# Part of an FFN's up projection as seven block products, three down chunks, the residual in DRAM, and new planner costs

## The chip, the cores and the metric

One core of a Trainium2 chip runs the whole program. The metric is the device time in microseconds (us) of one execution; the kernel before takes 1389.71 us, the median of three runs.

## The reference, cut to what matters

Two decoder layers on an input of 512 tokens x 1024 features, all in float32. Each layer is a mixer (layer 0: a gated state-space scan and stick-breaking attention; layer 1: an mLSTM) with a residual sum, followed by a gated conv FFN with a residual sum:

```python
def conv_ffn(h, up_w, conv_w, conv_b, down_w):
    u = causal_dwconv(h @ up_w, conv_w, conv_b)
    gate, val = jnp.split(u, 2, axis=-1)
    return (jax.nn.silu(gate) * val) @ down_w
...
        h = h + conv_ffn(rmsnorm(h, norm_w[layer, 1]), ffn_up_w[layer], ffn_conv_w[layer],
                         ffn_conv_b[layer], ffn_down_w[layer])
```

`up_w` is 1024 x 5632, that is 22 gate tiles and 22 value tiles of 128 features; `down_w` is 2816 x 1024. The conv has width 3.

## The kernel before, in words

Activations lie feature by token: a tile is 128 features x 512 tokens, the residual `h` is 8 such tiles. A float32 product is made of three fast ones (`mm3`): each operand is split into a rounded part hi (a cast on ACT) and the rest lo (a subtraction on VectorE, called DVE), and PE multiplies hi by hi, hi by lo and lo by hi. Weights come from DRAM as units of up to 128 x 1024 elements (`load_unit`, on SP's queue, into two `raw` buffers), are split in `split_weights` into tiles hi and lo with five buffers of each, and are asked for ahead by `prefetch`. All other tiles come from one pool of 71 slots.

The FFN (`ffn`, line 1174) follows the list `FFN_PLAN`. An entry "up" j makes the gate tile j and the value tile 22 + j: `feat` runs 8 x 3 matmuls of 512 columns for each; DVE reads the PSUM and multiplies it with the row `rb` of the norm, giving u; ACT scales u into c; DVE adds the other two taps of the conv; ACT takes the SiLU of the gate, and DVE multiplies the two. The result is one tile of the down projection's input.

The down projection takes tiles in chunks of 8 (0 to 7, 8 to 15). Within a chunk it uses a scheme of seven block products: two input tiles and two output tiles, with the 512 tokens halved, form a 2 x 2 block product, which seven products of 256 columns give in place of eight. `token_sums` makes the sums of token halves of a pair of tiles (F, G, and the splits B, s, Fh, Fl, Gh, Gl), once per pair; `weight_tiles` makes the sums of weight blocks: P1 and P3 by two DMAs each, the second of which accumulates and is issued by POOL, P2 and P4 by DVE. `down_blocks` (line 1227) runs the products for the two output tiles 2c and 2c + 1, for c of 0 to 3, and adds them to `h`, which stays in its slots, straight from PSUM. Three PSUM tiles are used, X, Z and Y; X takes four products one on top of the other and is read in between, Y two. So a product that goes on in X or Y has to wait for the reader of the one before. The tiles 16 to 21 go plainly (`down_rest`, six per output tile, 512 columns).

The order of instructions is set by a planner. `Recorder` collects all calls; `cost` (line 288) gives each a duration; `order` simulates the five engines, with latencies between them, buffers and PSUM, and always issues on each engine the earliest call in program order that is ready. The program is then written out in that order, fixed for each engine. The four lines below set how far weights can run ahead, and how many slots there are:

```python
W_BUFS = 5
RAW_BUFS = 2
SLOTS = 71
SLOT = 520
```

Of the kernel before, what the change touches and what calls it, by code (L numbers as in the profile page):

```python
# [84 lines left out]
def _ffn_units(i, l):  # L85
# [3 lines left out]
    for kind, n in FFN_PLAN:  # L89
        if kind == "up":  # L90
# [6 lines left out]
        else:  # L97
# [175 lines left out]
class Recorder:  # L273
# [15 lines left out]
    def cost(c):  # L289
# [25 lines left out]
        return 60 + 2.0 * n  # L315
# [133 lines left out]
class Net:  # L449
# [65 lines left out]
    def weight_tiles(self):  # L515

        v = self.nc.vector
        while self.wi < len(self.sizes):
# [655 lines left out]
    def ffn(self, l, h, last):  # L1174
        nc = self.nc
        xs, _, _, rb = self.norm(h, f"nw{l}1")
        pairs, ss, first = {}, [], None
        for kind, j in FFN_PLAN:
            if kind == "down":
                a, b = CHUNKS[j]  # L1180
                for c in range(4):
                    self.down_blocks([pairs[k] for k in range(a // 2, b // 2)], h, c)
                continue
            if kind == "rest":
                self.down_rest(ss, h, last)
                continue
            cc = []
            for part in range(2):
                n = j + part * FF
                ps = self.ps(("pj", "zz", "yy")[self.n % 3])  # L1190
                self.feat(ps, xs)
                u, c = self.slot("u"), self.slot("c")
                nc.vector.tensor_tensor(u, ps, rb, op=ALU.mult)
                nc.scalar.activation(c, u, AF.Identity, scale=self.param(f"fw{l}2", n), bias=self.param(f"fb{l}", n))
                for d in (1, 2):
                    nc.vector.scalar_tensor_tensor(c[:, d:T], u[:, 0 : T - d], self.param(f"fw{l}{2 - d}", n), c[:, d:T],
                                                   op0=ALU.mult, op1=ALU.add)
                cc.append(c)
            nc.scalar.activation(cc[0], cc[0], AF.Silu)
            nc.vector.tensor_tensor(cc[1], cc[0], cc[1], op=ALU.mult)  # L1200
# [7 lines left out]
    def token_sums(self, c1, c2):  # L1208
# [3 lines left out]
        t = self.slot("B11", F32R)  # L1212
        self.nc.scalar.copy(t[:, a], c1[:, a])
        v.tensor_tensor(t[:, b], c1[:, a], t[:, a].bitcast(F32), op=ALU.subtract)
# [269 lines left out]
```

## Time and profile before

| | us |
|---|---|
| median of 3 runs (1389.37 to 1391.11) | 1389.71 |
| the profiled execution | 1389.56 |
| its span, first to last instruction | 1387.8 |
| PE (TensorE matmuls) busy | 1376.7 |
| DVE (VectorE) busy | 1116.2 |
| ACT (ScalarE) busy | 783.9 |
| POOL (GpSimd) busy | 87.1 |

The granted TensorE clock was 1.000 over the span. The first FFN runs from about 453 to 811 us, the second from about 1026 to the end; before the first lie the state-space scan and the attention, between the two the mLSTM. Busy times of an engine are a union: where two instructions overlap, the time counts once, so the sum of their durations is longer. Matmuls overlap so much that only the distance of their starts says how fast they go. All matmuls and nearly all other instructions have the line of the helper that issues them, L436 (L446 in the changed kernel), so groups are told apart by their tiles.

### The profile page before, as it was taken

The numbers are of one execution on the slowest core, as the hardware profiler recorded it, in microseconds if no ns is written. First come the engines' busy times: TensorE is split into PE (matmuls) and PEld (weight loads), VectorE is DVE, ScalarE is ACT, GpSimd is POOL, SyncE is SP. The second block draws the span as 40 slices with busy tenths as digits, with TensorE's granted clock in tenths as the row PEclk, the third lists the DMA queues.
The fourth block names the chain that finished last, engine by engine and source line by source line (L and its number), as shares of the span: only waits on it lengthen the run. The fifth ranks groups of instructions, "written<-read, shape, count | busy, mean of one in ns | idle before, by whom it ended". The sixth has DMA issues, their size and how long they took to land.

```text
span 1387.8 us, 20206 instructions
## 1 busy us (share of the span) xinstructions
PE 1376.7 (99%) x7491; PEld 1185.3 (85%) x7491; DVE 1116.2 (80%) x1963; ACT 783.9 (56%) x1325; POOL 87.1 (6%) x172
## 2 busy tenths in 40 slices
PE   9999999999999999999999999999999999999998
PEld 8898998989788888988898898888888899889887
DVE  7999889999997778878877657798758886888662
ACT  7798997786665444344434446776434444444440
POOL 0000001201120001000100000110000010010000
PEclk9999999999999999999999999999999999999999
DMA  6423223223312345243532225222234354443422
GB/s 220 130 77 112 86 78 98 70 83 132 98 46 91 101 127 137 92 138 113 129 122 95 81 82 171 77 92 89 65 106 126 102 129 129 122 133 95 137 68 84
DMA packets 53617, 147.96 MB, mean 107 GB/s; under 512 B 6136, under 2 KB 7160, under 8 KB 53520
## 3 DMA queue, kind: packets, MB, share of 16 engines
q1 hardware_dynamic: 48912, 138.29, 31.4%
q0 software_dynamic: 4608, 8.39, 3.7%
q8 instruction: 59, 0.97, 0.3%
q14 instruction: 38, 0.31, 0.1%
HBM read 141.36 MB, written 2.15 MB: 103 GB/s over the span
## 4 chain that ended last, share of the span: by engine, by line
PE 88%; DVE 5%; issue 3%; ACT 3%; POOL 1%; DMA 0%; SPq 0%; DVEq 0%; POOLq 0%; ACTq 0%
PE pj L436 43%; PE yy L436 26%; PE zz L436 14%; PE tt L436 5%; DVE gt L436 1%; DVE wt L436 1%; DVE lo L436 1%; DVE wTl L436 0%; ACT L436 0%; ACT Kh L436 0%; DMA h<-in_xT 0%; POOL wt L436 0%; ACT Q L436 0%; DVE ss L436 0%; ACT hi L436 0%
## 5 line engine op out<-in xcount | busy, mean ns | idle before, releaser
L436 ACT CAST hi<-raw 128x1024 fp32r<-128x1024 f32 (+2 forms) x236 | 227.8, 968 | 257.2 <-PE yy L436 58.6
L436 DVE TENSOR_TENSOR lo<-raw,hi 128x1024 fp32r<-128x1024 f32 (+2 forms) x236 | 263.8, 1120 | 25.2 <-ACT hi L436 24.5
L436 PE MATMUL pj<-xnh,hi 128*128 128x512 f32 x488 | 194.1, 398 | 0.0
L436 PE MATMUL pj<-xnh,lo 128*128 128x512 f32 x488 | 193.9, 397 | 0.0
L436 PE MATMUL pj<-xnl,hi 128*128 128x512 f32 x488 | 193.5, 396 | 0.0
L436 DVE SCALAR_TENSOR_TENSOR c<-u,pp,c 128x511 f32<-128x511 f32 (+2 forms) x212 | 158.0, 748 | 3.9 <-ACT c L436 1.6
L436 PE MATMUL yy<-xnl,hi 128*128 128x512 f32 x320 | 126.4, 395 | 0.0
L436 PE MATMUL yy<-xnh,lo 128*128 128x512 f32 x320 | 126.2, 394 | 0.0
L436 PE MATMUL yy<-xnh,hi 128*128 128x512 f32 x320 | 125.6, 392 | 0.0
L436 PE MATMUL pj<-lo,xnh 128*128 128x384 f32 (+2 forms) x320 | 108.6, 340 | 0.0
L436 PEld LDWEIGHTS pj<-xnh,lo 128*128 128x128 f32 x488 | 91.8, 188 | 19.1
L436 PEld LDWEIGHTS pj<-xnl,hi 128*128 128x128 f32 x488 | 91.8, 188 | 18.9
L436 PEld LDWEIGHTS pj<-xnh,hi 128*128 128x128 f32 x488 | 91.9, 188 | 18.8 <-issue 0.2
L436 PE MATMUL pj<-hi,xnl 128*128 128x384 f32 (+2 forms) x320 | 107.2, 336 | 0.0
L436 PE MATMUL pj<-hi,xnh 128*128 128x384 f32 (+2 forms) x320 | 106.8, 338 | 0.0
L436 ACT ACTIVATE c<-u,pp 128x512 f32<-128x512 f32 x100 | 81.1, 813 | 9.7 <-DVE u L436 8.3
L436 PE MATMUL zz<-xnl,hi 128*128 128x512 f32 x184 | 72.7, 395 | 0.0
L436 PE MATMUL zz<-xnh,lo 128*128 128x512 f32 x184 | 72.5, 394 | 0.0
L436 PE MATMUL zz<-xnh,hi 128*128 128x512 f32 x184 | 72.2, 392 | 0.0
L436 PEld LDWEIGHTS yy<-xnh,hi 128*128 128x128 f32 x320 | 60.2, 188 | 14.0
L436 PEld LDWEIGHTS yy<-xnl,hi 128*128 128x128 f32 x320 | 60.1, 188 | 13.9
L436 PEld LDWEIGHTS yy<-xnh,lo 128*128 128x128 f32 x320 | 60.1, 188 | 13.3
(418 smaller groups left out, 3330.7 us busy)
## 6 DMA issues: line engine op xcount, KB each, us to landing
raw<-in_w SPq DMA_DIRECT2D x168, 512.0 KB, 3.4
raw<-in_w SPq DMA_DIRECT2D x44, 384.0 KB, 3.1
P<-in_w SPq DMA_DIRECT2D x32, 256.0 KB, 5.6
P<-in_w POOLq DMA_DIRECT2D x32, 256.0 KB, 6.8
h<-in_xT SPq DMA_DIRECT2D x16, 256.0 KB, 4.7
E<-acsd SPq DMA_DIRECT2D x16, 256.0 KB, 3.9
raw<-in_w SPq DMA_DIRECT2D x16, 256.0 KB, 3.1
raw<-in_w SPq DMA_DIRECT2D x8, 264.0 KB, 2.7
```

The source lines that it names most:

```text
L436: getattr(getattr(nc, c.engine), c.method)(*(r(a) for a in c.args), **{k: r(v) for k, v in c.kw.items()})
```

## The change

It does five things.

1. In each FFN five of the 22 gate/value pairs (7, 10, 13, 16, 19) are made in block form: the two output tiles are gate j and value j, the inputs the eight feature tiles in four pairs. `up_blocks` copies four of the seven products from PSUM with ACT (two of them negated), adds or subtracts three with DVE, and then multiplies both u with `rb`. The sums of the input's token halves (entries "x" of the plan) need the weighted input itself, `hw`, which DVE makes anew; two of the seven operands are the splits that there are already.
2. The down projection has three chunks of 6 tiles (0 to 5, 6 to 11, 12 to 17), so three tile pairs per product, and four tiles are left for `down_rest`.
3. The residual lies in DRAM during the FFN (`hd`): 8 tiles are stored after the norm, each chunk loads two tiles per set and stores them again, and `down_rest` loads all eight.
4. The weight units of a block are as wide as the block needs (`raw` and P tiles of 768, 384 or 1024, 512 columns).
5. The planner's costs are changed: matmuls 0.4414 ns per column and 5 ns, scans 2.04 ns per element, POOL's power 250 + 190 ns per element, masks 330 + 0.6 ns.

```diff
-CHUNKS = [(0, 8), (8, 16)]
-REST = 16
-FFN_PLAN = [("up", j) for j in range(9)] + [("down", 0)] + [("up", j) for j in range(9, 17)] + [("down", 1)]
-FFN_PLAN += [("up", j) for j in range(17, FF)] + [("rest", 0)]
+CHUNKS = [(0, 6), (6, 12), (12, 18)]
+REST = 18
+UP_BLOCKS = (7, 10, 13, 16, 19)
+FFN_PLAN = [("up", 0), ("up", 1), ("x", 0), ("up", 2), ("x", 1), ("up", 3), ("x", 2), ("up", 4), ("x", 3), ("up", 5)]
+FFN_PLAN += [("load", 0), ("up", 6), ("down", 0)] + [("up", j) for j in range(7, 12)]
+FFN_PLAN += [("load", 1), ("up", 12), ("down", 1)] + [("up", j) for j in range(13, 18)]
+FFN_PLAN += [("load", 2), ("up", 18), ("down", 2)] + [("up", j) for j in range(19, FF)] + [("rest", 0)]
...
             if c.ins[0].base.dt == F32R:
-                return max(n / 2.4 + 2.5, m * 0.84)
-            return max(4 * n / 2.4 + 5, 3.4 * m)
+                return max(n * 0.4414 + 5, m * 0.84)
+            return max(4 * n * 0.4414 + 5, 3.4 * m)
...
+            if c.method == "tensor_tensor_scan":
+                rate = 2.04
...
-        return 60 + 2.0 * n
+        if c.method == "tensor_tensor":
+            return 250 + 190 * n
+        return 330 + 0.6 * n if c.method == "affine_select" else 100
...
-            r1, r2 = self.raw_tile(), self.raw_tile()[:, 0:kb]
+            r1, r2 = self.raw_tile()[:, 0 : 2 * kb], self.raw_tile()[:, 0:kb]
...
-            p1, p2, p3, p4 = (self.slot(f"P{k}") for k in (1, 2, 3, 4))
+            p1, p2, p3, p4 = (self.slot(f"P{k}", n=kb) for k in (1, 2, 3, 4))
...
+        hd = [self.dram.tile([P, T], F32, name=self.name("hd")) for _ in range(KD)]
+        for k in range(KD):
+            nc.sync.dma_start(hd[k], h[k])
...
+        def load(c):
+            loaded[c] = self.slot("h"), self.slot("h")
+            for e in range(2):
+                nc.sync.dma_start(loaded[c][e], hd[2 * c + e])
...
+            if kind == "x":
+                hw = []
+                for k in (2 * j, 2 * j + 1):
+                    hw.append(self.slot("hw"))
+                    v.tensor_scalar(hw[-1], h[k], self.param(f"nw{l}1", k), None, op0=ALU.mult)
+                xb.append(self.token_sums(*hw, xs[2 * j], xs[2 * j + 1]))
...
                 for c in range(4):
-                    self.down_blocks([pairs[k] for k in range(a // 2, b // 2)], h, c)
+                    if c < 3:
+                        load(c + 1)
+                    self.down_blocks([pairs[k] for k in range(a // 2, b // 2)], *loaded[c], c)
+                    for e in range(2):
+                        nc.sync.dma_start(hd[2 * c + e], loaded[c][e])
...
+    def blocks(self, xs, c, read):
...
+        X, Z, Y = (self.ps(t)[:, 0:n] for t in (("pj", "yy", "zz"), ("yy", "pj", "pj"))[c % 2])
+        steps = (X, "11", "X1"), (Z, "21", "Z"), (X, "n2", "X2"), (Y, "n1", "Y1"), (X, "t3", "X3"), (Y, "22", "Y2"), (X, "t4", "X4")
...
+    def up_blocks(self, xs, rb, c):
...
+            if name in ("X1", "X2"):
+                nc.scalar.copy(u1[:, a if name == "X1" else b], ps)
+            elif name in ("Y1", "X4"):
+                nc.scalar.activation(u2[:, b if name == "Y1" else a], ps, AF.Copy, scale=-1.0)
+            elif name == "X3":
+                v.tensor_tensor(u2[:, b], u2[:, b], ps, op=ALU.subtract)
+            else:
+                o = u1[:, a if name == "Z" else b]
+                v.tensor_tensor(o, o, ps, op=ALU.add)
...
+        for u in (u1, u2):
+            v.tensor_tensor(u, u, rb, op=ALU.mult)
```

What this does to the order shows at two places. The first is DVE in the first FFN, where a gate/value pair is read from PSUM (u), with its weights' lo between and its conv (c) behind. Before, one ordinary pair; every pair looks so:

```order
L436 TENSOR_TENSOR u_5893<-pj_5847,rb_5481 128x512
L436 TENSOR_TENSOR B_1252_5886<-c_5860,B_1252_5886 128x256
L436 TENSOR_TENSOR lo_5903<-raw_5830,hi_5890 128x1024
L436 SCALAR_TENSOR_TENSOR c_5901<-u_5893,pp,c_5901 128x511
L436 SCALAR_TENSOR_TENSOR c_5901<-u_5893,pp,c_5901 128x510
L436 TENSOR_TENSOR u_5932<-pj_5888,rb_5481 128x512
L436 TENSOR_TENSOR lo_5938<-raw_5867,hi_5927 128x1024
L436 SCALAR_TENSOR_TENSOR c_5941<-u_5932,pp,c_5941 128x511
L436 SCALAR_TENSOR_TENSOR c_5941<-u_5932,pp,c_5941 128x510
L436 TENSOR_TENSOR c_5941<-c_5901,c_5941 128x512
```

In the changed kernel, the end of the first block pair (7), whose reads stand among the last lo of its own weights and those of the next pairs:

```order
L446 TENSOR_TENSOR lo_6609<-raw_6535,hi_6590 128x1024
L446 TENSOR_TENSOR u_6604<-u_6604,pj_6532 128x256
L446 TENSOR_TENSOR lo_6659<-raw_6600,hi_6644 128x1024
L446 TENSOR_TENSOR u_6654<-u_6654,yy_6529 128x256
L446 TENSOR_TENSOR lo_6683<-raw_6627,hi_6668 128x1024
L446 TENSOR_TENSOR u_6604<-u_6604,pj_6612 128x256
L446 TENSOR_TENSOR u_6604<-u_6604,rb_5546 128x512
L446 TENSOR_TENSOR u_6654<-u_6654,rb_5546 128x512
L446 SCALAR_TENSOR_TENSOR c_6707<-u_6604,pp,c_6707 128x511
L446 SCALAR_TENSOR_TENSOR c_6707<-u_6604,pp,c_6707 128x510
```

One read per tile and one product with `rb` in it have become three short reads (`u<-u` with a PSUM tile), each behind a lo of 1024 columns, and two products with `rb`; four further reads are ACT's.

The second place is PE in the last chunk of the first FFN, between the second product in X (moving tiles Fh, Fl) and the third (Gh, Gl), which may start when the second has been read. Before, X is `pj_7618`:

```order
L436 MATMUL pj_7618<-Fh_7378,lo_7603 128x256
L436 MATMUL zz_7707<-Fl_7390,hi_7590 128x256
L436 MATMUL zz_7707<-Fh_7378,lo_7603 128x256
L436 MATMUL yy_7741<-B_1386_6305,hi_7676 128x256 [waits Activation_49]
L436 MATMUL yy_7741<-B_1386_6305,hi_7676 128x256
L436 MATMUL yy_7741<-B_1386_6305,lo_7696 128x256
L436 MATMUL yy_7741<-B_1419_6925,hi_7676 128x256 x2
L436 MATMUL yy_7741<-B_1419_6925,lo_7696 128x256
L436 MATMUL yy_7741<-B_1452_7090,hi_7676 128x256 x2
L436 MATMUL yy_7741<-B_1452_7090,lo_7696 128x256
L436 MATMUL pj_7618<-Gh_6850,hi_7624 128x256 [waits DVE_49]
```

In the changed kernel X is `yy_8398`:

```order
L446 MATMUL yy_8398<-Fh_8288,lo_8400 128x256
L446 MATMUL pj_8462<-Fh_8091,hi_8382 128x256
L446 MATMUL pj_8462<-Fl_8105,hi_8382 128x256
L446 MATMUL pj_8462<-Fh_8091,lo_8400 128x256
L446 MATMUL pj_8462<-Fh_8288,hi_8382 128x256
L446 MATMUL pj_8462<-Fl_8299,hi_8382 128x256
L446 MATMUL pj_8462<-Fh_8288,lo_8400 128x256
L446 MATMUL pj_8513<-B_1603_7537,hi_8497 128x256 [waits Activation_49]
L446 MATMUL yy_8398<-Gh_7901,hi_8396 128x256 [waits DVE_49]
```

With three tile pairs per product in place of four, 7 matmuls of 256 columns stand between the two, where it was 11 (a row with x2 is two); it is the closest such place in each order. In all the changed order has 576 matmuls of 512 columns fewer and 1008 of 256 columns more, and 284 more instructions on DVE, 142 per FFN.

## Rows read from the trace of the kernel before

**Rows 1.** The page: the span, and busy time of PE and DVE.
```profile
span 1387.8 us, 20206 instructions
...
PE 1376.7 (99%) x7491; PEld 1185.3 (85%) x7491; DVE 1116.2 (80%) x1963; ACT 783.9 (56%) x1325; POOL 87.1 (6%) x172
```

**Rows 2.** Stretches: window, length, busy PE, PEld, DVE, ACT, POOL, clock, DMA.
```profile
453.00:811.00 358.00, 358.00 (x1885) 305.94 (x1884) 277.17 (x422) 159.12 (x223) 16.52 (x41) 1.00 0.39 112
1026.00:1388.00 362.00, 358.16 (x1883) 305.60 (x1881) 266.85 (x406) 148.25 (x205) 15.30 (x17) 1.00 0.38 111
200.00:425.00 225.00, 221.30 (x1291) 193.85 (x1290) 208.91 (x394) 160.79 (x314) 36.27 (x65) 1.00 0.27 83
900.00:975.00 75.00, 73.57 (x399) 61.17 (x399) 68.17 (x181) 50.71 (x113) 10.55 (x26) 1.00 0.26 85
...
520.00:595.00 75.00, 75.00 (x489) 68.42 (x488) 62.73 (x106) 32.65 (x48) 5.26 (x6) 1.00 0.43 115
```

**Rows 3.** The chain that ended last: start, us, engine, tile, matmuls.
```profile
469.94 66.64 PE pj L436 x288
...
580.33 1.07 PE yy L436 x9
...
732.94 11.11 PE yy L436 x48
...
785.70 4.16 PE yy L436 x18
```

**Rows 4.** VectorE's groups by form: busy us, mean ns, idle before.
```profile
L436 DVE TENSOR_TENSOR lo<-raw,hi 128x1024 fp32r<-128x1024 f32 x168 | 205.2, 1224 | 19.5 <-ACT hi L436 19.2
...
L436 DVE TENSOR_TENSOR lo<-P,hi 128x512 fp32r<-128x512 f32 x64 | 43.4, 686 | 3.9 <-ACT hi L436 3.7
L436 DVE TENSOR_TENSOR lo<-raw,hi 128x768 fp32r<-128x768 f32 x44 | 41.9, 953 | 1.1 <-ACT hi L436 1.0
...
L436 DVE COPY rep<-rstd 128x512 f32<-128x512 f32 x5 | 2.1, 426 | 4.5 <-POOL rstd L436 4.5
```

**Rows 5.** VectorE's timeline in the first FFN: start, us, operation.
```profile
510.94 1.54 DVE L436 SCALAR_TENSOR_TENSOR c<-u,pp,c 128x511 f32<-128x511 f32 x2
512.51 0.69 DVE L436 TENSOR_TENSOR c<-c,c 128x512 f32<-128x512 f32 x1
...
565.56 1.22 DVE L436 TENSOR_TENSOR lo<-raw,hi 128x1024 fp32r<-128x1024 f32 x1
566.70 0.69 DVE L436 TENSOR_TENSOR lo<-P,hi 128x512 fp32r<-128x512 f32 x1
567.30 0.41 DVE L436 TENSOR_TENSOR h<-h,pj 128x256 f32<-128x256 f32 x1
567.64 0.42 DVE L436 TENSOR_TENSOR h<-h,yy 128x256 f32<-128x256 f32 x1
```

**Rows 6.** DMA: two queues and one issue in 525 to 555, then the page's.
```profile
q0 software_dynamic: 864, 1.57, 34.6%
q1 hardware_dynamic: 1315, 2.67, 26.6%
...
raw<-in_w SPq DMA_DIRECT2D x1, 512.0 KB, 4.7
...
raw<-in_w SPq DMA_DIRECT2D x168, 512.0 KB, 3.4
```

**Rows 7.** Groups that the planner's new costs are about: scan, power, mask.
```profile
L436 DVE TENSOR_TENSOR_SCAN gt<-gt,cc 128x383 f32<-128x383 f32 x16 | 15.4, 960 | 1.0 <-ACT gt L436 1.0
...
L436 POOL TENSOR_SCALAR_AFFINE_SELECT wt<-wt 128x128 f32<-128x128 f32 x64 | 35.3, 563 | 231.8 <-ACT wt L436 201.1 <-DVE kqs L436 11.9 <-PE tt L436 8.9
...
L436 POOL TENSOR_TENSOR f<-ss,mhalf 128x4 f32<-128x4 f32 x8 | 8.1, 1007 | 65.1 <-DVE ss L436 65.1
```

More of the change, by code (lines that the diff above doesn't have):

```diff
@@ L89, in _ffn_units @@
     for kind, n in FFN_PLAN:
-        if kind == "up":
+        if kind == "up" and n in UP_BLOCKS:
+            u.append(np.stack([up[m][:, k::2] for m in (n, FF + n) for k in range(2)], axis=1))
+        elif kind == "up":
             u += [up[n], up[FF + n]]
@@ L1222, in token_sums @@
         gs = self.split(g, "G")
-        half = lambda t, s: (t[0][:, s], t[1][:, s])
-        return {"11": (t[:, a], t[:, b]), "21": half(s2, a), "22": half(s2, b),
+        return {"11": s11, "21": half(s2, a), "22": half(s2, b),
                 "n1": half(fs, a), "n2": half(fs, b), "t3": half(gs, a), "t4": half(gs, b)}
-    def down_blocks(self, xs, h, c):
-        v = self.nc.vector
+    def blocks(self, xs, c, read):
         kb, n = len(xs) * P, T // 2
-        a, b = slice(0, n), slice(n, T)
         X, Z, Y = (self.ps(t)[:, 0:n] for t in (("pj", "yy", "zz"), ("yy", "pj", "pj"))[c % 2])
-        h1, h2 = h[2 * c], h[2 * c + 1]
-        at = {"i": 0, "u": None}
-        def product(ps, form, more=False):
-            i = at["i"]
+        steps = (X, "11", "X1"), (Z, "21", "Z"), (X, "n2", "X2"), (Y, "n1", "Y1"), (X, "t3", "X3"), (Y, "22", "Y2"), (X, "t4", "X4")
+        for i, (ps, form, name) in enumerate(steps):
             if i % 2 == 0:
-                at["u"] = self.unit()
-            hi, lo = at["u"]
-            at["i"] = i + 1
+                hi, lo = self.unit()
+            more = name[1:] > "1"
             for k, x in enumerate(xs):
@@ L1247, in product, with down_blocks, read, down_rest @@
                 self.mm3(ps, (hi[:, s], lo[:, s]), x[form], not more and k == 0, k == len(xs) - 1, skip_group_check=more)
-        add = lambda o, ps, op=ALU.add: v.tensor_tensor(o, o, ps, op=op)
-        product(X, "11")
-        product(Z, "21")
-        add(h1[:, a], X)
-        product(X, "n2", True)
-        add(h1[:, a], Z)
-        product(Y, "n1")
-        add(h1[:, b], X)
-        product(X, "t3", True)
-        add(h2[:, b], Y, ALU.subtract)
-        product(Y, "22", True)
-        add(h2[:, b], X, ALU.subtract)
-        product(X, "t4", True)
-        add(h1[:, b], Y)
-        add(h2[:, a], X, ALU.subtract)
-    def down_rest(self, ss, h, last):
-        nc = self.nc
-        for c in range(8):
+            read(name, ps)
+    def down_blocks(self, xs, h1, h2, c):
+        a, b = slice(0, T // 2), slice(T // 2, T)
+        to = {"X1": h1[:, a], "Z": h1[:, a], "X2": h1[:, b], "Y2": h1[:, b], "Y1": h2[:, b], "X3": h2[:, b], "X4": h2[:, a]}
+        def read(name, ps):
+            op = ALU.add if name in ("X1", "Z", "X2", "Y2") else ALU.subtract
+            self.nc.vector.tensor_tensor(to[name], to[name], ps, op=op)
+        self.blocks(xs, c, read)
+    def up_blocks(self, xs, rb, c):
+        nc, v = self.nc, self.nc.vector
+        a, b = slice(0, T // 2), slice(T // 2, T)
+        u1, u2 = self.slot("u"), self.slot("u")
+        def read(name, ps):
+            if name in ("X1", "X2"):
[4 more added lines that the diff above has]
+                v.tensor_tensor(u2[:, b], u2[:, b], ps, op=ALU.subtract)
+            else:
+                o = u1[:, a if name == "Z" else b]
+                v.tensor_tensor(o, o, ps, op=ALU.add)
+        self.blocks(xs, c, read)
+        for u in (u1, u2):
+            v.tensor_tensor(u, u, rb, op=ALU.mult)
+        return u1, u2
+    def down_rest(self, ss, hd, last):
+        nc, h = self.nc, [self.slot("h") for _ in range(KD)]
+        for c in range(KD):
+            nc.sync.dma_start(h[c], hd[c])
+        for c in range(KD):
             ps = self.ps(("pj", "zz", "yy", "tt")[c % 4])
@@ L1272, in down_rest @@
                 nc.sync.dma_start(self.out[c], h[c])
+        return h
     def load_x(self, a=0, b=KD):
@@ L1377, in run @@
         S.clear()
-        self.ffn(0, h, False)
+        h = self.ffn(0, h, False)
         xs, var, r, rb = self.norm(h, "nw10")
```

47 lines of the change are left out of this document (28 added, 19 removed).

## The prediction

> **What bounds the kernel now.** I read the page's busy times first: PE works 1376.7 of 1387.8 us and VectorE (DVE) 1116.2 [rows 1]. So the time is a sum of matmuls, unless another engine keeps PE waiting. Then the table by stretch [rows 2]: in the first FFN (453 to 811) PE is busy in all of 358.00 us, and DVE in 277.17 (77%); in the second PE is short by 3.84 of 362, the end of the kernel, where the last sum and store follow the last matmul. So an FFN has no wait that a better order could save; only fewer or shorter matmuls shorten it. Elsewhere there is a little: PE lacks 3.70 us in 200 to 425 (attention, DVE 208.91 of 225, 93%) and 1.43 us in 900 to 975 (mLSTM).
>
> Since matmuls overlap, the mean duration of one says nothing of its rate. The chain that ended last gives that [rows 3]: 288 matmuls of 512 columns in 66.64 us are 231.4 ns each; one gate/value pair is 48 of them in 11.11; a product of a down block of 256 columns runs 9 in 1.07 us, so 118.5 ns each; 18 of the rest's matmuls take 4.16.
>
> **What PE saves.** A pair in block form has 7 products x 4 tile pairs x 3 = 84 matmuls of 256 columns in place of 48 of 512: 84 x 0.1185 = 9.95 us against 11.11, 1.15 saved. Five pairs in two layers: 11.5 us. Of the down projection two more of the 22 feature tiles go into blocks (18 in place of 16). Three chunks of 6 tiles have 4 sets x 7 x 3 x 3 = 252 matmuls each, 29.9 us; before it was two chunks of 4 x 84, 39.8 each; the rest shrinks from 8 x 18 to 8 x 12 matmuls of 512. Per layer: 3 x 29.9 + 22.2 = 111.8 against 79.6 + 33.3 = 113.0, 1.15 us less, 2.3 in two. **PE's gain is 13.8 us.** Both orders bear out the count: 576 matmuls of 512 columns fewer and 1008 of 256 more. This lies on the path wholly, as PE has no gap there.
>
> **What DVE pays.** Its instructions overlap a little: starts behind one another are 1.14 us apart for 1024 columns, 0.60 for 512 and 0.34 for 256 [rows 5], some 85 ns less than the durations [rows 4]; two taps of the conv in a row, the second of which needs the first, take 1.57 [rows 5]. The lo of 768 columns goes by 0.95 - 0.085 = 0.87, of 384 by 0.47, halfway between 0.34 and 0.60. Per layer:
> - A pair in blocks drops two lo of 1024 and two reads with rb (3.48) and adds one lo of 1024, five of 512, two sums of weights, three reads of 256 columns and two multiplications with rb (7.56): +4.08, five times +20.4. The conv stays.
> - The sums of the normalised input are 4 x (four of 256 and two of 512) = 10.2. The eight scaled copies hw have no row; a copy of 512 columns takes 0.43 and a subtraction 0.69 [rows 4], so with the overlap off they cost 2.7 to 4.8; I take 2.7, since the copy too has one tensor to read. Together +13.0.
> - A down set was 1.14 + 7 x 0.60 + 7 x 0.34 = 7.72, eight of them 61.8. Now it is 0.87 + 7 x 0.47 + 7 x 0.34 = 6.54, and twelve 78.5: +16.7.
> - The rest's eight lo go from 768 to 512 columns, -2.1; pair 16/17 gets sums in place of two splits, +2.3.
>
> That is +50.3 us (142 instructions, as the order has), 62.4 if none overlapped. DVE would have 277.2 + 50.3 = 327.5 of the 351.1 us that PE then needs: 93%, up from 77%. **The cover is nearly used up**, and it isn't even. An ordinary pair costs two lo, two reads, two conv pairs and a product, 2.28 + 1.20 + 3.14 + 0.60 = 7.2; a block pair 11.3; the sums of two tiles 5 x 0.34 + 3 x 0.60 = 3.5. So pairs 7 to 11 give DVE some 55 us (two at 11.3, three at 7.2, three sets of sums) beside 53.2 of PE, whereas pair 6 and the first chunk give it 7.2 + 26.2 beside 41.0. Five weight buffers let DVE run ahead from the one into the other, but not far.
>
> The price is bounded by two rows. At 77% over the FFN, and 84% in 520 to 595, PE loses nothing; at 93% in 200 to 425 it loses 3.70 in 225, which over 351 us is 5.8 per layer, 11.5 in all [rows 2]. I take 2 per layer, **+4 us**: nearer to zero, because there DVE holds a chain (scan, product, transpose) for which PE waits at once, and here mostly weights that can be made early.
>
> The order shows a smaller form of the same. A block's second product is written into the PSUM tile that the first reader has just added. Before, at least 11 matmuls (1.30 us) stood between; now at one place per layer it is 7 (0.83 us), and at seven more 10 (1.19). The read takes 0.41 [rows 5], and the engine reading it may first have to end a lo of 1.14. With 0.3 us lost at each of the 16 it would be 5 us; it is inside the bound above.
>
> **What costs nothing.** ACT has 159 of 358 us in an FFN [rows 2]; its casts grow like DVE's lo, and four reads of 256 columns per block pair come on top, some 25 to 30 us a layer: half full. POOL issues 68 accumulating transfers in place of 32, and is busy in only 16.5 of 358 us [rows 2]. The residual in DRAM is 32 loads and 32 stores of 0.26 MB a layer on SP; between a tile's store and its next load lies the better part of a stage. But SP's queue is in order: a store of h waits for the chunk's last sums, and weight loads stand behind it. If the sums are on time the loads are too. If transfers are late, that is a rival below.
>
> **The planner.** New costs change the order everywhere. A scan over 383 columns was put at 0.47 us and now at 0.85, traced 0.96; a power at 0.07, now 1.01, traced 1.01; a mask of 128 columns at 0.32, now 0.41, traced 0.56 [rows 7]. All move towards the trace, so waits in the two stretches with gaps should shrink. At most 5.1 us (3.70 + 1.43) is there to gain; a worse order might lose as much. DVE at 93% stays as it is, so I take **-2**.
>
> **The sum** against the profiled execution (1389.56, span 1387.8, 0.15 below the median of the runs, 1389.71): 1389.6 - 13.8 + 4 - 2 = **1377.8 us**. From 0.2% (2.8 us) on I call it faster or slower.
>
> **A rule weighed.** DVE's 512-column form has a mean of 686 ns, but starts 0.60 us apart [rows 4, 5]. [...] A kernel in which every instruction cost its whole duration would have 327.5 + 564 x 0.085 = 375 us of DVE per layer, 24 over PE, and end at 1389.6 - 13.8 + 49 = 1424.5. By the spacing of rows 5 it doesn't; I leave this 0.01.
>
> **The rivals.**
> - DVE becomes the bound (slower). At a sustained share s a layer takes 327.5 / s; below s = 91.5% that is more than the 358 of now. At 90% it is 363.9, 12.8 over PE, and the time 1389.6 - 13.8 - 2 + 25.6 = 1399.4. For it: no FFN stretch shows over 84%, and pairs 7 to 11 and 13 to 17 ask for over 100% for 53 us each. Against it: 93% is held for 225 us in attention [rows 2]. 0.09.
> - Transfers become the bound in the chunks (no change). Pair 6 with a chunk moves 4 sets x 7 x 0.197 MB of weight blocks, 1.05 of the pair's and 16 x 0.262 of h, 10.7 MB in 41 us; 8 x 0.197 = 1.6 of it accumulates. In 525 to 555 six accumulating transfers held the DMA engines for 34.6% of 30 us, 1.7 us each, and 2.67 MB of others for 26.6%, 3.0 us per MB [rows 6]; the chunk's eight smaller ones (1.3 each) and 9.1 MB make 38 of 41 us. A raw tile of 512 KB then lands in 4.7 us [rows 6], not in the median of 3.4 [rows 6]; with two raw buffers, 1.3 us late in every other of 24 sets is 15.6, and the time about 1389.6 - 13.8 - 2 + 15.6 = 1389.4. Against it: P tiles can be fetched a stage before. 0.07.
> - The new costs don't do what they should, and the mixers lose as much as they might gain: 1389.6 - 13.8 + 4 + 5 = 1384.8. 0.08.
>
> **How the numbers follow.** My forecast gets 0.75. Faster: forecast and the third rival, 0.83; same: the second, 0.07; slower: the first, and the case in which nothing overlaps, 0.10. The range goes from 1369 (no new wait, all 5.1 us regained gives 1370.7, and a little for tighter spacing) to 1390, which takes in the stall bound of 11.5 (1387) and the second rival; it leaves out the other two.
>
> **What would show it.** PE busy near 1363 us, 512-column matmuls still 0.231 and those of 256 columns 0.1185 apart; DVE 320 to 330 us in each FFN of about 351; PE short by 1 to 4 us within each, in pairs 7 to 11 and 13 to 17, with DVE (lo, or a u or h read) as what it waited for; in the mixers fewer waits on wt and num. I am wrong if PE waits on lo in every chunk with raw behind it (transfers), if an FFN takes over 358 us (DVE), or if 256-column matmuls run slower than 118.5 ns when their moving data is the normalised input.

## The result and the profile after

The change is slower. It takes **1429.05 us** (median of 4 runs, 1427.27 to 1434.2) against 1389.62 of the kernel before on the same chip: ratio 1.029, 95% interval 1.026 to 1.0315. Forecast were 1377.8 us and a range of 1369 to 1390. The profiled execution took 1427.27 us.

The page of the changed kernel: the span, busy times, and the chain by engine.

```profile
span 1425.5 us, 22026 instructions
...
PE 1380.7 (97%) x7923; PEld 1207.4 (85%) x7923; DVE 1201.3 (84%) x2249; ACT 831.5 (58%) x1472; POOL 125.9 (9%) x208
...
PE 72%; DMA 10%; DVE 10%; ACT 3%; issue 3%; SPq 0%; POOL 0%; DVEq 0%; ACTq 0%; POOLq 0%
```

PE was busy in all but 11 us of the span before [rows 1]; now 45 us lack. Part of the chain that ended last are now DMAs (10%) and DVE (10%). Before, its shares were:

```profile
PE 88%; DVE 5%; issue 3%; ACT 3%; POOL 1%; DMA 0%; SPq 0%; DVEq 0%; POOLq 0%; ACTq 0%
```

The table by stretch says where (columns as in [rows 2]):

```profile
550.00:575.00 25.00, 21.82 (x169) 21.62 (x170) 16.75 (x34) 7.71 (x14) 3.22 (x4) 0.93 0.74 197
600.00:625.00 25.00, 25.00 (x151) 22.13 (x150) 24.56 (x41) 14.24 (x23) 0.00 (x0) 1.00 0.40 130
700.00:725.00 25.00, 25.00 (x150) 22.13 (x149) 24.93 (x41) 14.86 (x24) 0.00 (x0) 1.00 0.47 150
1150.00:1175.00 25.00, 21.71 (x143) 20.84 (x144) 15.24 (x26) 8.93 (x15) 1.74 (x2) 0.86 0.69 200
1250.00:1275.00 25.00, 19.63 (x158) 18.79 (x157) 13.37 (x25) 8.57 (x14) 1.74 (x2) 1.00 0.75 207
1350.00:1375.00 25.00, 20.99 (x150) 20.51 (x151) 13.91 (x28) 8.58 (x15) 0.87 (x1) 0.86 0.78 236
```

Nearly all of the loss lies in the chunks of the down projection and the block pair behind each. In the four stretches shown that lose, DVE works only 13 to 17 of 25 us (18.4 and 19.6 in 650 to 675 and 750 to 775, which lose 4.0 and 3.5), while the DMA engines are busy for 0.69 to 0.78 of the time. Between the chunks, where I had looked for the loss, DVE works 24.56 and 24.93 of 25 us, and PE lacks nothing.

How a gap comes about shows in the chain of the first FFN, 552 to 563 us (start, us, what):

```profile
552.02 6.77 DMA raw<-in_w
...
558.88 0.10 DVE P L446
...
559.49 0.41 DVE h L446
559.90 0.47 DVE lo L446
560.37 0.34 DVE h L446
560.71 0.14 issue
560.85 1.68 PE yy L446 x9
```

and in DVE's and PE's own timelines there (start, us, operation; in brackets the idle time before and what ended it):

```profile
555.45 0.41 DVE L446 TENSOR_TENSOR h<-h,pj 128x256 f32<-128x256 f32 x1
558.88 0.69 DVE L446 TENSOR_TENSOR P<-P,raw 128x512 f32<-128x512 f32 x1 [3.02 <-DMA raw<-in_w]
559.49 0.41 DVE L446 TENSOR_TENSOR h<-h,zz 128x256 f32<-128x256 f32 x1
...
560.29 0.41 DVE L446 TENSOR_TENSOR h<-h,yy 128x256 f32<-128x256 f32 x1
```

```profile
560.85 0.36 PE L446 MATMUL yy<-Fh,hi 128*128 128x256 f32 x1 [2.72 <-DVE h L446]
```

A raw tile of the block pair's weights lands after 6.77 us. In-order DVE waits 3.02 us for it with a sum of weights that PE needs only later; behind that sum stand the reads of PSUM into `h`, for which PE waits 2.72 us. So here a late transfer of weights for later stops the product of now.

**One account of the whole.** The distance from each matmul's start to the next was compared with the median that this shape has in the kernel before; the differences, summed over the program, are called gaps; they are worked out from the starts in the trace. A lead is the time from POOL's issue of the first accumulating transfer of a set (P1) to DVE's sum that reads it (P2); the median over all sets is shown. Times are medians of the runs, the rest is of the profiled execution, all in us.

```
                                       time    span   gaps  span - gaps  lead
before                                1389.6  1387.8  30.9    1356.9     24.2
e3  new planner costs alone           1393.1  1390.4  33.5    1356.9     23.9
e8  e3 + residual in DRAM             1394.0  1391.5  34.7    1356.8     23.4
e7  e3 + chunks of 6                  1388.3  1386.3  31.5    1354.8     31.6
e12 e7 + residual in DRAM             1388.1  1386.9  32.4    1354.5     31.4
e13 e7 + 16 slots held                1389.9  1389.2  34.7    1354.5     11.8
e14 e12 + 16 slots held               1387.2  1386.1  31.6    1354.5     14.4
e1  e7 + block pairs                  1402.0  1399.2  56.2    1343.0      8.6
e17 e1, 12 slots given back           1381.5  1381.5  38.5    1343.0     23.1
after (e1 + residual in DRAM)         1429.1  1425.5  82.5    1343.0      9.3
e18 after, 12 slots given back        1391.9  1388.4  45.4    1343.0     29.0
```

Span less gaps falls from 1356.9 to 1343.0, by 13.9 us. By the way gaps are made this is the count of matmuls at the distances of before, so it repeats the forecast's 13.8 and doesn't test it. What tests it is that the distances stayed: their medians are 118 ns for 256 columns and 231 for 512 before, 118 and 232 in the changed kernel; and in e17 (below), which has the same matmuls and few gaps, PE is busy for 1365.8 us, where 1363 were forecast. So the loss is new gaps, 51.6 us of them.

### The profile page after: what moved, and what is told of

It reads as the page before. It is cut to its first block, busy times and chain, and to the rows that moved or that the text cites. A ratio compares the mean times of both kernels' runs of the same rounds, so it can differ in the third digit from the quotient of the medians.

```text
span 1425.5 us, 22026 instructions
## 1 busy us (share of the span) xinstructions
PE 1380.7 (97%) x7923; PEld 1207.4 (85%) x7923; DVE 1201.3 (84%) x2249; ACT 831.5 (58%) x1472; POOL 125.9 (9%) x208
## 2 busy tenths in 40 slices
DMA packets 84733, 191.09 MB, mean 134 GB/s; under 512 B 9592, under 2 KB 25976, under 8 KB 84624
## 4 chain that ended last, share of the span: by engine, by line
PE 72%; DMA 10%; DVE 10%; ACT 3%; issue 3%; SPq 0%; POOL 0%; DVEq 0%; ACTq 0%; POOLq 0%
PE pj L446 41%; PE yy L446 16%; PE zz L446 11%; DMA raw<-in_w 6%; PE tt L446 4%; DMA P<-in_w 3%; DVE lo L446 3%; DVE h L446 1%; DVE gt L446 1%; ACT hi L446 1%; ACT E L446 1%; DVE wt L446 1%; ACT Kh L446 1%; DMA E<-mrow 0%; DVE wTl L446 0%
## 5 line engine op out<-in xcount | busy, mean ns | idle before, releaser
L446 ACT CAST hi<-raw 128x1024 fp32r<-128x1024 f32 (+3 forms) x252 | 225.0, 897 | 233.9 <-DMA raw<-in_w 95.3
L446 DVE TENSOR_TENSOR lo<-raw,hi 128x1024 fp32r<-128x1024 f32 (+3 forms) x252 | 258.9, 1029 | 44.6 <-ACT hi L446 44.1
L446 PE MATMUL pj<-xnh,hi 128*128 128x512 f32 (+1 forms) x592 | 230.3, 389 | 7.3 <-ACT u L446 7.3
L446 PE MATMUL pj<-xnh,lo 128*128 128x512 f32 (+1 forms) x592 | 228.1, 386 | 0.0
L446 PE MATMUL pj<-xnl,hi 128*128 128x512 f32 (+1 forms) x592 | 227.6, 384 | 0.0
L446 ACT CAST hi<-P 128x384 fp32r<-128x384 f32 (+1 forms) x136 | 69.3, 540 | 60.4 <-PE zz L446 18.8
L446 DVE TENSOR_TENSOR lo<-P,hi 128x384 fp32r<-128x384 f32 (+1 forms) x136 | 77.9, 591 | 1.7 <-ACT hi L446 1.6
L446 PE MATMUL yy<-xnh,lo 128*128 128x512 f32 (+1 forms) x200 | 75.3, 377 | 3.1 <-DVE lo L446 3.1
L446 PE MATMUL yy<-xnh,hi 128*128 128x512 f32 (+1 forms) x200 | 75.4, 377 | 2.9 <-ACT hi L446 2.9
L446 PE MATMUL yy<-xnl,hi 128*128 128x512 f32 (+1 forms) x200 | 74.9, 374 | 0.0
```

The costliest lines, as they stand in the source:

```text
L446: getattr(getattr(nc, c.engine), c.method)(*(r(a) for a in c.args), **{k: r(v) for k, v in c.kw.items()})
```

## The experiments

Theories at first: T, the traffic of `h` makes weight loads land late, and two raw buffers give them no room; Q, a store of `h` in SP's in-order queue waits for DVE's sums, and weight loads stand behind it; D, DVE is too full; P, the planner's new costs. Each run is the changed kernel, or the kernel before, with the edit shown; those with new costs and chunks and without block pairs are the changed kernel with `UP_BLOCKS = ()`.

### The parts one by one

**e1: the residual stays in its slots.**

```diff
-        for k in range(KD):
-            nc.sync.dma_start(hd[k], h[k])
...
-            loaded[c] = self.slot("h"), self.slot("h")
-            for e in range(2):
-                nc.sync.dma_start(loaded[c][e], hd[2 * c + e])
+            loaded[c] = h[2 * c], h[2 * c + 1]
...
-                    for e in range(2):
-                        nc.sync.dma_start(hd[2 * c + e], loaded[c][e])
...
-                return self.down_rest(ss, hd, last)
+                return self.down_rest(ss, h, last)
```

> The change with the residual kept in its eight slots, as before: no store and no load of h in an FFN, everything else as in the change. Theory T (the h traffic makes the raw weight loads land late, and with two raw buffers the chunk waits for them): raw of 512 KB lands in about 3.3 us again, PE's gaps in the six chunk stretches go, 1372 to 1385 us. Theory Q (h stores on SP's queue wait for the sums and hold the weight loads behind them) says the same. Theory D (VectorE has too much to do) and theory P (the planner's new costs) expect 1415 us or more.

Measured: 1402.02 us, ratio 1.0098 (1.0075 to 1.012). So the residual in DRAM takes 27 us of the 39, and what is left is still 12 over the kernel before, 26 more than PE's gain allows. This lies between what T and Q and what D and P expected: none of them is the whole cause.

**e2: the changed kernel with three raw buffers.**

```diff
-RAW_BUFS = 2
+RAW_BUFS = 3
```

> The change with a third raw buffer. T: a late landing is partly hidden, about half of the loss comes back, 1395 to 1412 us. Q: the loads still stand behind the stores, 1420 us or more. D and P: 1420 to 1430, nothing changes.

Measured: 1417.88, ratio 1.0202 (1.0182 to 1.0222); 11 us come back, fewer than T expected and more than the others did.

**e3: the kernel before with the new planner costs alone.**

> The kernel before with the planner's new costs alone. P: slower by 20 us or more. T, Q and D: within 5 us of before, 1384 to 1394; a few us faster if the waits in attention and mLSTM shrink as I forecast.

Measured: 1393.06, ratio 1.0023 (1.0013 to 1.0033). P falls: 3.4 us of loss, not 39, but no gain either.

**e4: the changed kernel with the stores of `h` on POOL's queue**, behind the norm and behind each set.

```diff
-            nc.sync.dma_start(hd[k], h[k])
+            nc.gpsimd.dma_start(hd[k], h[k])
...
-                        nc.sync.dma_start(hd[2 * c + e], loaded[c][e])
+                        nc.gpsimd.dma_start(hd[2 * c + e], loaded[c][e])
```

> The change with the stores of h issued on POOL's queue instead of SP's; the loads of h and all bytes stay. Q: weight loads are no longer held, 1380 to 1400 us. T: same bytes at the same time, 1420 to 1432. D and P: 1420 to 1432.

Measured: 1412.81, ratio 1.0167 (1.0151 to 1.0184): 16 of the 27 us come back by the queue alone, bytes unchanged. That is less than Q expected and more than the others did. SP's waits show it, the changed kernel first, then e4 (engine, waited for: us, times, longest):

```profile
SPq L446 <- DVE h L446: 198.8, 87, 16.8
```

```profile
SPq L446 <- DVE h L446: 126.5, 43, 6.5
```

In the changed kernel the stores wait for DVE's sums with weight loads behind them on the same queue; on another queue the same stores took 16 us less.

**e7: chunks of 6, 6, 6, no block pairs, residual in slots, new costs**, that is e1 with

```diff
-UP_BLOCKS = (7, 10, 13, 16, 19)
+UP_BLOCKS = ()
```

and without the entries "x" of the plan.

> No up projection in blocks; the down projection in chunks of 6, 6, 6, the residual kept on chip, the new planner costs. Against before PE saves 2.3 us by the prediction's count, and the new costs alone took 3.4 more (e3). Theory L or B: sets of 7.5 us are too short for the chain raw, P, sums, raw, so that gaps open in the six chunks as in e1: time 1394 to 1402. Theory D (DVE falls by some 33 us per layer against e1): no gaps in the chunks, time 1388 to 1393.

Measured: 1388.28, ratio 0.999 (0.9981 to 1.0): 4.8 below e3 (in the spans 4.1: 2.1 by the count of matmuls, 2.0 of gaps). The chunks of 6 are harmless.

**e8: only the residual in DRAM**, with `CHUNKS = [(0, 8), (8, 16)]`, `REST = 16` and `UP_BLOCKS = ()` in the changed kernel.

> Only the residual in DRAM: chunks of 8, 8, no up projection in blocks, the new planner costs, 24 loads and 24 stores of h per layer where the whole change has 32 and 32. PE does the work of before. If the stores and loads of h cost by themselves, as they do in the whole change (27 us by e1, six chunks): some two thirds of it, time 1405 to 1413. If they cost only where the sets are short (7.5 us, not 10): 1392 to 1398, what the new costs take and a few us.

Measured: 1394.01, ratio 1.0034 (1.0021 to 1.0047), 1 us above e3. **e12: chunks of 6 with the residual in DRAM:**

> Chunks of 6, 6, 6 with the residual in DRAM and no up projection in blocks (e7, 1388.3, has the residual on chip). All 32 loads and 32 stores of h per layer are there, VectorE has some 33 us less per layer than in the change. Q and D together: 1388 to 1393. T (the transfers in a chunk of 6 are too many, whatever VectorE does): 1403 to 1415.

Measured: 1388.09, ratio 0.9985 (0.9976 to 0.9995), level with e7. T falls: the 33.6 MB of `h` (191.09 MB moved in the changed kernel, 157.51 in e1) cost nothing where no pair is in blocks.

So the parts don't add up. Chunks and costs give -1, the block pairs +14 on top (where -11.5 was forecast), and DRAM +27, but only on top of the block pairs.

### What the block pairs lose

**e5: e1 with three raw buffers.** L: a set holds both raw buffers until its sums are made. B: the accumulating transfers are late.

> The change with the residual kept on chip (as e1, 1402.0 us, span 1399.2, where successive matmul starts lie 56.2 us further apart in all than the median step of their shape, against 30.9 before) and with three buffers for raw weights in place of two. Theory L (a block set holds both raw buffers until its sums are made, so the next set's loads, 4 to 6 us each, start too late for sets of 7.5 us): most of the 25 us of new gaps goes, time 1381 to 1390, ACT and DVE wait for raw under 25 us in all in the FFNs. Theory D (VectorE is full, 24.4 to 24.7 of 25 us in the pairs between the chunks): the gaps stay, time 1398 to 1404. Theory B (the accumulating P transfers, 6.4 us to landing, are what is late): little change, 1395 to 1402, with P and no longer raw as what DVE waits for.

Measured: 1399.4, ratio 1.0076 (1.0059 to 1.0092); not told apart from e1. L alone falls. DVE's waits for transfers only changed sides. In e1 its sums of P waited so:

```profile
DVE P L446 <- DMA raw<-in_w: 14.6, 12, 2.9
...
DVE P L446 <- DMA P<-in_w: 1.9, 1, 1.9
```

and in e5, with no wait for raw left,

```profile
DVE P L446 <- DMA P<-in_w: 17.3, 6, 4.5
```

**e6: e1 with the planner's transfers costed as they land.**

```diff
-                end = start + 2000 + cost
+                end = start + 4500 + cost
...
-                end = start + 4500
+                end = start + 6500
```

> The change with the residual kept on chip (as e1) and with the planner's transfers costed as they land in the chunks: 4.5 us plus the size's share in place of 2.0 for a load, 6.5 in place of 4.5 for an accumulating one. Nothing else is changed. Theory L or B with the order at fault (the planner puts DVE's weight work where it thinks the transfers have landed, and the in-order engine then waits with the PSUM readers behind it): PE's waits on lo, hi and u in the chunks shrink, time 1388 to 1397. If the buffers alone set when a load starts (L without the order) or VectorE is full (D): 1398 to 1406.

Measured: 1403.83, ratio 1.0103 (1.0088 to 1.0118): no gain; that the planner takes transfers for faster than they are isn't the cause.

**e9: e1 with `UP_BLOCKS = (9, 15, 19, 20, 21)`**, and **e10, the same with the residual in DRAM.** U: each block pair loses by itself, wherever it is.

> The change with the residual kept on chip (e1, 1402.0) and with its five block pairs at other places: one between two chunks (9 and 15) and three behind the last chunk (19, 20, 21), where e1 has two, two and one (7, 10, 13, 16, 19). The work of every engine is the same. Theory D (two block pairs between two chunks ask for more of VectorE than the time has, 54.7 us beside 53.2 of PE by the prediction's terms, so that it comes into the next chunk without a lead; with one it is 50.6 beside 54.4): the gaps of e1 go, time 1376 to 1384. Theory U (each block pair costs by itself, wherever it stands: its first readers are on ACT, in order behind casts that wait for raw): gaps stay, time 1394 to 1404.

> The whole change, residual in DRAM, with the block pairs at 9, 15, 19, 20, 21 as in e9. DRAM took 27 us more with the pairs where the change has them (e1 against the change), but 1 us with no block pair and chunks of 8 (e8 against e3). If a store of h holds the loads behind it only where VectorE is late with the sums (Q and D together): e9 plus 1 to 6 us, 1378 to 1390. If it is the chunks of 6 with their short sets, or the transfers' total (T): e9 plus 15 to 27, 1393 to 1408.

Measured: e9 1403.86, ratio 1.0094 (1.0078 to 1.011), e10 1406.83, ratio 1.0117 (1.0102 to 1.0132). With one block pair between two chunks, where DVE has room, the same work as a whole loses as much as in e1: D falls in the form that it had. The gaps moved with the pairs, though. At the first two chunks of each layer they are 8.8 us in all (one pair between two chunks) where e1 has 16.1 (two), at the last chunk, with three pairs behind it, 18.5 where e1 has 9.2 (one). And DRAM takes 3 us there, not 27, so its price hangs on where the block pairs stand: the change has one right behind each of the three chunks, e10 only behind the last.

**e11: e1 with one tap of the conv left out in pairs 6 to 18.**

```diff
-                for d in (1, 2):
+                for d in (1, 2)[: 1 if 6 <= j <= 18 else 2]:
```

> e1 (change, residual kept on chip, block pairs at their places), with the last of the three taps of the FFN's convolution left out in pairs 6 to 18: 26 instructions of 511 or 510 columns per layer less on VectorE, some 0.7 us each, 18 us per layer, of them 7 between two chunks. PE, ACT, the transfers and the places of the block pairs stay. Theory D: the gaps go, time 1376 to 1386. Theory U, or L (the weight pipe): time 1395 to 1403.

Measured: 1401.36, ratio 1.0075 (1.0057 to 1.0092). DVE is busy for 15 us less per layer (1168.7 in all, 1198.9 in e1; 18 were expected), and nothing changes that the intervals could tell. That rules out D a second time.

### Slots

What was left: the sums of the normalised input hold 16 of the 71 slots from pairs 1 to 4 until pair 19. P tiles come from the same slots. POOL's timeline from 440 to 552 us shows when it issued the accumulating transfers of the first chunk's four sets, two for each. In e7, without block pairs:

```profile
454.48 1.06 POOL L446 DMA_DIRECT2D P<-in_w  x1 [37.02 <-DVE acc L446]
457.39 0.87 POOL L446 DMA_DIRECT2D P<-in_w  x1 [1.85 <-PE tt L446]
498.04 0.92 POOL L446 DMA_DIRECT2D P<-in_w  x1 [38.17 <-DMA P<-in_w]
504.06 2.64 POOL L446 DMA_DIRECT2D P<-in_w  x3 [5.11 <-DMA P<-in_w]
514.02 1.75 POOL L446 DMA_DIRECT2D P<-in_w  x2 [7.31 <-DMA P<-in_w]
```

In e1, the last row of which is the first block pair's:

```profile
493.19 1.97 POOL L446 DMA_DIRECT2D P<-in_w  x2 [32.39 <-DMA P<-in_w]
522.23 1.76 POOL L446 DMA_DIRECT2D P<-in_w  x2 [27.07 <-DVE lo L446]
529.22 0.86 POOL L446 DMA_DIRECT2D P<-in_w  x1 [5.23 <-DVE c L446]
531.31 0.86 POOL L446 DMA_DIRECT2D P<-in_w  x1 [1.22 <-DVE u L446]
541.12 0.86 POOL L446 DMA_DIRECT2D P<-in_w  x1 [8.95 <-ACT hi L446]
542.95 0.86 POOL L446 DMA_DIRECT2D P<-in_w  x1 [0.95 <-DVE lo L446]
549.25 1.76 POOL L446 DMA_DIRECT2D P<-in_w  x2 [5.44 <-DVE h L446]
```

In e7 all eight are issued by 516 us, and from 498 us on what POOL's waits end with is a plain load into a P tile. In e1 the last is issued at 543, and from 522 us on the waits end with instructions that work on other tiles (lo, c, u, hi, h); that these are the readers which give the slots free is inferred. The median lead falls from 31.6 to 8.6 us; an accumulating transfer alone takes 4.4 us to land there (192 KB) or 6.5 (256 KB), by the page of e1.

**e13: e7 with 16 slots held and no other work; e14: the same with the residual in DRAM.**

```diff
+                for k in range(4):
+                    xb.append(self.slot("xb"))
+                    nc.gpsimd.memset(xb[-1][:, 0:1], 0.0)
...
+            for t in xb if j == 19 else ():
+                v.tensor_tensor(t[:, 0:1], t[:, 0:1], cc[1][:, 0:1], op=ALU.add)
```

> e7 (1388.3: chunks of 6, residual on chip, no block pair) with 16 slots written in one column where the change makes the sums of the normalised input (pairs 1 to 4), and held until pair 19, where sixteen additions of one column end their use: no other work, and these columns enter no result. Theory S (the slots that the sums hold keep the P tiles from being fetched early): the lead of the accumulating transfers before their sum falls from a median of 31 us to under 12, gaps open at the chunks as in e1, time 1396 to 1413. Theory U (the block pairs' own readers and transfers): the gaps don't come, 1387 to 1391.

> e12 (1388.1: chunks of 6, residual in DRAM, no block pair) with the same 16 slots held. If what DRAM took on top of e1 (27 us) comes from few slots and the in-order queue (its loads and stores wait, weights behind them): slower than e13, up to 27 us. If it comes with the block pairs next to the chunks alone (e10, with the pairs moved, was only 3 us above e9): e13 or, since DRAM gives eight slots back, less: 1388 to e13.

Measured: e13 1389.87, ratio 1.0 (0.9991 to 1.0009); e14 1387.16, ratio 0.9979 (0.997 to 0.9988). Half of theory S is shown: held slots alone bring the lead from 31.6 down to 11.8 us. The other half fell in that form: short leads alone cost 1.6 us, not 8 to 25. e14 came out 0.8 below the least that was expected, so DRAM takes nothing on top of held slots alone.

**e17: e1, e18: the whole change, with the sums of the first pair of input tiles used for all four.** PE's work, weights, transfers and places stay, 12 slots are free.

```diff
+            if kind == "x" and j:
+                xb.append(dict(xb[0], **{"11": ..., "21": ..., "22": ...}))
+                continue
```

> e1 (change, residual kept on chip, 1402.0) with the sums of the normalised input made for the first pair of its tiles alone and used for all four: left out are six of the eight scaled copies, twelve of sixteen sums and their splits per layer, so 12 of the 16 held slots are free, and VectorE has some 10 us less per layer (18 us less changed nothing in e11). PE's matmuls, the weights, the transfers and the places of the block pairs stay. Theory S with U (few slots and the block pairs' doubled stream of weights only together open the gaps): leads of the accumulating transfers back above 15 us, most of the 25 us gone, 1376 to 1386. Theory U alone (the loop raw, sums, raw of a block pair is longer than its 9.95 us of PE whatever the slots): 1394 to 1402.

> The whole change (1429.05) with the same sums left out and 12 slots free. If the slots are behind both parts of the loss: 1376 to 1390. If the h stores in SP's queue next to the block pairs cost their 27 us whatever the slots: e17 plus 15 to 27. Theory U alone: 1415 to 1430.

Measured: e17 **1381.5**, ratio 0.9935 (0.9918 to 0.9951); e18 **1391.87**, ratio 1.0013 (1.0002 to 1.0024). Giving 12 slots back takes 20.5 us off e1 and 37 off the whole change; e18 lies 1.9 above what the slots alone were to leave, and 10 above e17. POOL's timeline of e17 in the same stretch:

```profile
460.43 1.06 POOL L446 DMA_DIRECT2D P<-in_w  x1
463.64 0.87 POOL L446 DMA_DIRECT2D P<-in_w  x1 [2.15 <-DMA P<-in_w]
503.70 1.75 POOL L446 DMA_DIRECT2D P<-in_w  x2 [39.19 <-DMA P<-in_w]
514.53 4.43 POOL L446 DMA_DIRECT2D P<-in_w  x5 [9.08 <-DMA P<-in_w]
519.49 0.87 POOL L446 DMA_DIRECT2D P<-in_w  x1 [0.53 <-DMA P<-in_w]
```

The chunk's eight and the block pair's two are issued before 521 us, and the median lead is 23.1 us again.

**What follows.** Without the residual in DRAM it takes both together, few slots and block pairs, as four runs with the same chunks and costs show: neither 1388.3 (e7), few slots alone 1389.9 (e13), block pairs with most slots given back 1381.5 (e17, 4 are still held), both 1402.0 (e1). What a block pair adds can be counted, though that it is the reason is argued and not shown: its weights are 7 x 512 = 3584 columns to be split in 9.95 us of PE, 360 per us, as in a chunk (2688 in 7.47), where an ordinary pair has 2048 in 11.11, 184 per us. Behind a chunk an ordinary pair would let the weight path catch up, and a block pair wouldn't. That is at most a part: e9 keeps half of the gaps at the first two chunks, though ordinary pairs stand right behind them. e17 also relieves DVE by 7.8 us per layer (busy 1183.3, e1 1198.9) and ACT by 2.7, early in the FFN; since e11 took 15 off DVE for nothing, I put its gain down to the slots. A run with all the work and more slots was not made.

DRAM's 27 us are made of 16 that the place of the stores in SP's queue explains (e4; some 6 of them are the lower clock of the last section, by an estimate from the traces: one such stretch in e4's, five in the changed kernel's) and 11 that stay open; with the slots given back DRAM takes 10 (e18 against e17), without block pairs none. That the stores wait for DVE's sums, which wait behind weights that are late already, fits all of this; a run that shows it by itself was not made.

### A version that beats both

**e15: chunks of 6 with the old costs (e7 with the costs of the kernel before); e16: with the residual in DRAM too.**

> Before with one part of the change alone: chunks of 6, 6, 6, the residual on chip, no block pairs, the old planner costs. PE saves 2.3 us by the prediction's count (2.1 by the matmul steps of e7). The new costs took 3.4 us in e3, and e7 stands 4.8 below e3. If the parts add up: 1384 to 1386. If the old costs (a scan, a power, a mask, and a matmul's duration too short) go ill with the smaller chunks: 1387 to 1391.

> The same as e15 with the residual in DRAM (e12 with the old costs). e12 and e7 are level, so e15 within 1 us, 1384 to 1387; above 1390 if the old order puts the stores of h ahead of weight loads where the new one doesn't.

Measured: e15 1390.08, ratio 1.0006 (0.9997 to 1.0015), e16 1390.41, ratio 1.0005 (0.9996 to 1.0014). So the parts don't add up, and the second case came: with chunks of 6 the new costs are worth about 2 us, with chunks of 8 they lose 3.4. What beats the kernel before, by little, is chunks of 6 with the residual in DRAM and the new costs, without block pairs (e12, 0.9985, interval below 1). (e14, the same with 16 slots held, measured 0.9 less still, but the intervals overlap; e17 leaves sums out and is no version.) Leaving out the block pairs alone turns 39 us of loss into 1.5 of gain.

## Why the prediction was wrong, step by step

- **What PE saves, 13.8 us:** right. The matmuls are as counted and start as far apart as before. PE's busy time is 1380.7 us and not near 1363, some 8 of the difference by the lower clock (last section); in e17 it is 1365.8.
- **What DVE pays:** near. I had 50.3 us more per layer by spacing, 100.6 in all; DVE is busy for 85.1 more. But the step built on it, that the cover is nearly used up and the risk lies in pairs 7 to 11, was wrong: at 24.9 of 25 us of DVE PE lost nothing, and the +4 of stall was put at the wrong place. The stretches [rows 2] had shown attention losing 3.70 us at 93%; I took the share for the cause.
- **"If the sums are on time the loads are too":** the step that failed. It costs the residual in DRAM at nothing, as it is in e8, e12 and e14, and the block pairs' transfers too. The sums were not on time: they are DVE instructions that stand behind sums of weights whose raw tile was late, as the chain shows; SP's waits for DVE's `h` (198.8 us in all) are the way back to the loads. Put at nothing, the residual in DRAM took 27 us here: 16 by the place of the stores in SP's queue, and 11 whose cause stays open.
- **What is missing from the sum altogether:** slots. I wrote that P tiles can be fetched a stage before, against the rival on transfers. In the kernel before they are (lead 24.2 us). But the text counted durations and bytes, and never that the sums of the input hold 16 of 71 slots from pairs 1 to 4 until pair 19, out of which those early P tiles come. The description of the kernel had both facts: all other tiles come from one pool of 71 slots, and the sums are made in pairs 1 to 4. This was worth about 20 us in e1 and 37 in the change (by e17 and e18, with 12 of the 16 given back). It overlaps the 27 of the step before: with the slots given back DRAM takes 10.
- **The rival "transfers become the bound in the chunks"** had the right place and the right look (raw behind lo and the sums, in every chunk), but not the size: 15.6 us against 51.6 of new gaps. It took every other set as late by what a busier DMA adds, 1.3 us. Measured in 530 to 580, a raw tile of 512 KB lands in 6.8 us, 3.4 more than the page's median of before [rows 6], and the loss goes on from there: DVE's reads behind it, then SP's queue behind those, then the clock, at half behind five of PE's waits (last section).

```profile
raw<-in_w SPq DMA_DIRECT2D x5, 512.0 KB, 6.8
hd<-h SPq DMA_DIRECT2D x8, 256.0 KB, 4.6
```

- **DVE becomes the bound:** wrong; e11 speaks against it, and so do the stretches with DVE at 99%. Its sign, an FFN of over 358 us, came all the same, for the other reason: the two take some 373 and 385.
- **What was to show me wrong,** PE waiting on lo in every chunk with raw behind it, came nearly so: raw is behind it, but PE waits more for the reads of PSUM than for hi and lo, since the reads stand behind the same sums and casts. The third sign didn't come: matmuls of 256 columns with the normalised input start 118 ns apart in the median. PE's longest waits in the changed kernel (us, times, longest):

```profile
PE yy L446 <- DVE h L446: 11.2, 4, 3.3
PE pj L446 <- ACT u L446: 7.3, 4, 2.4
PE pj L446 <- DVE h L446: 5.7, 8, 1.6
PE yy L446 <- DVE lo L446: 3.1, 2, 2.1
PE yy L446 <- ACT hi L446: 2.9, 1, 2.9
```

- **The planner, -2:** wrong sign, +3.4 by e3. The attention gained as forecast: in 200 to 425 PE lacks 1.51 us in e3 (busy 223.49 of 225) where it lacked 3.70 [rows 2], and its gaps shrink by 4.0. The first 200 us lost 2.5 of that, and the two FFNs some 4, in small pieces. The +3.4 are inside the bound of 5.1, but they are not the third rival: the mixers together lost nothing.
- **The rule weighed** (a DVE instruction costs its whole duration): its time, 1424.5, comes within 5 us of the measurement for a wrong reason. PE did not wait for a full DVE, as the stretches that lost most show.

## What to carry to other kernels

Count buffers like time: for each new tile write down from when to when it holds a slot, and ask whose early fetch used that slot. A transfer that is hidden is hidden by its lead; measure the lead (issue to first use; here 24.2 us in the median before, 9.3 after) before a change, and ask what shortens it. Here in-order DVE makes weights for later and also reads the results of now, and a late load stopped both (DVE for 3.02 us, PE for 2.72, at 558 us). Parts that were free or nearly so by themselves cost much together: held slots took 1.6 us alone (e13), block pairs with most slots given back none (e17), both 13.7 (e1), and the residual in DRAM, level without block pairs (e12), 27 more.

## What the runs showed of the hardware that I had not expected

**Behind five waits of PE the clock fell to half.** After the wait from 1165 us on (2.44 us, for ACT's `u`) PE ran at full speed for 1.2 us, and then at half: matmuls of 256 columns start 0.21 us apart in place of 0.12. Stretches of 1 us, columns as before, the granted clock being the third number from the end:

```profile
1167.97 0.39 PE L446 MATMUL pj<-xnh,hi 128*128 128x256 f32 x1 [2.44 <-ACT u L446]
1168.20 0.28 PE L446 MATMUL pj<-xnl,hi 128*128 128x256 f32 x1
...
1170.20 0.41 PE L446 MATMUL yy<-Gh,hi 128*128 128x256 f32 x1
1170.41 0.41 PE L446 MATMUL yy<-Gl,hi 128*128 128x256 f32 x1
```

```profile
1167.00:1168.00 1.00, 0.03 (x1) 0.03 (x1) 0.33 (x1) 0.92 (x2) 0.00 (x0) 1.00 0.20 82
...
1170.00:1171.00 1.00, 1.00 (x5) 0.90 (x5) 1.00 (x2) 0.00 (x0) 0.00 (x0) 0.50 0.77 242
...
1173.00:1174.00 1.00, 1.00 (x6) 0.83 (x5) 0.70 (x2) 1.00 (x3) 0.00 (x0) 1.00 0.73 295
```

After its first 20 us the changed kernel has five such stretches, 3.2 to 5.1 us long by the starts of the matmuls, each behind a wait of 2.25 to 3.03 us; together they cost some 8 us over the full rate, of the 51.6. The kernel before shows a clock of 1.00 in every 1 us of its span, and e17 a mean of 1.000 over its own. The longest wait was not followed by one,

```profile
1256.05 0.36 PE L446 MATMUL yy<-Fh,hi 128*128 128x256 f32 x1 [3.32 <-DVE h L446]
```

and the clock was 1.00 in each 1 us from 1256 to 1260. In e1, where PE waited for no engine longer than 1.5 us, it was 0.93 over 1325 to 1350 us. So what brings the lower clock on is not shown.

**DVE at 99% was harmless, and DVE at 56% not.** PE lost nothing beside DVE at 24.93 of 25 us (700 to 725), and 4 us beside 13.91 (1350 to 1375). Where the waits could be followed, as at 558 us, what counted was which instruction stood at its head.
